# Layer 0's expert stage: when the fetched rows of the second expert table are multiplied

## The chip, the cores and the metric

One core of a Trainium2 chip runs one program. Its engines work in parallel and wait for each other through semaphores: PE (TensorE, matmuls into PSUM), DVE (VectorE), ACT (ScalarE), POOL (GpSimd) and SP (SyncE, here only a queue that issues transfers). Sixteen DMA engines carry all transfers. The metric is the device time of one execution in microseconds (us), lower is better.

## What is computed

Two layers; each is a token mixer followed by an expert layer (PEER). Only layer 0's expert layer matters here. It handles 256 latent tokens and 256 context tokens, 1024 wide. For every token, 8 heads pick 16 of 16384 experts each; an expert is one row of a first table (u) and one row of a second table (v):

```
q = t @ w_q                                    # 8 heads, two half keys each
best, pos = top_k(cand, 16); eidx = ...        # 128 experts per token
g = softmax(best)
act = gelu(einsum("thkd,td->thk", u_tab[eidx], t))
w = g * act
out = einsum("thk,thkd->td", w, v_tab[eidx])   # this document's subject
x = x + gate * out
```

## The kernel before

In layer 0 one half of the tokens (the latents, called "own" here) is computed densely: all 16384 experts, with the unchosen ones given weight zero. The other half (the context, called "far" in the code) is computed from rows that are fetched one by one with indirect DMAs on POOL's queue. The two are interleaved in one program whose order is written out by hand; every engine runs its instructions in that order.

The layer's stages, by items that `run` calls one after the other:

- `up(i)`, 128 items: the dense product with the first table, one block of 128 experts each. Beside it run the top-k of all tokens and `far_up`, which fetches rows of the first table (`u_rows`).
- `experts(t4)`, 64 items, the **selection stage**: four tokens each. `one_hots` (lines 1346 to 1352) makes masks on ACT, DVE and POOL, two items ahead; PE multiplies them into `psG` (line 1364, four matmuls); DVE multiplies the result into `A` (line 1366).
- `down(i)`, 128 blocks in 127 items, the **down stage**: the dense product with the second table, 24 matmuls a block (lines 200 to 202, into `acc`). Its 512 KB of table come in by SP's queue (line 113, tiles `raw`, three deep) and are split into a high and a low part (`whl`, lines 174 to 178, five deep).

The far half's product with the second table is `far_down`: 64 **steps**. A step needs four gathers of 128 rows (`fetch`, line 1219, four POOL instructions) into a set of four buffers; DVE spreads the weights (`wl`, line 1401) and PE does eight matmuls into `psC` (line 1413). The rows of the next step are ordered from inside the step: ahead of the step's matmuls if they go to another set of buffers, behind them if they go to the same set. There are three sets: `own` (in traces `hb`), `lent` (in traces `fetched`; these are the buffers of `whl`, so the down stage can't split its table before they are given back) and, from down block 16 on, rows 0 to 15 of `A`, which the down stage has used up by then. So in the selection stage two sets alternate; from there to block 16 there is one set alone; after that two again. After step 31 and after step 63, sixteen tile columns are moved out, transposed (`psX`, line 1429) and added to the context stream. The move behind step 31 is held back until block 28 (line 1421), as it writes into `A`. Behind step 63 come statistics and normalisation for layer 1 (`far_end`).

`far_go(want)` advances `far_down` until it has yielded `want` times; the first yield only orders the rows of step 0. `EARLY` is the number of steps that run in the selection stage, 24 in layer 0 (6 in layer 1). `far_go` is called at the end of each item: line 1373 in the selection stage, with at most one step more than before, and line 1506 in the down stage.

Of the kernel before, what the change touches and what calls it, by code (L numbers as in the profile page):

```python
# [69 lines left out]
class Builder:  # L70
# [10 lines left out]
    LO_DOWN = "v"  # L81


    FAR, WQ, UP, SHARE, EARLY = (256, 96), (8.0, 3.5), (4.0, 1.9), (0.75, 0.6), (24, 6)

    def __init__(self, tc, t, out):
        self.tc, self.nc, self.t, self.out = tc, tc.nc, t, out
# [919 lines left out]
    def peer(self, l, seg, far):  # L1007
# [8 lines left out]
        two = far != seg  # L1016
        NF = self.FAR[l]
        off = 0 if two else NF
        N = S - off
# [4 lines left out]
        EARLY = self.EARLY[l]  # L1024
# [3 lines left out]
        hold = dict(i=-1)  # L1028
# [71 lines left out]
        def psT(shape, name):  # L1100
            return self.ps.tile(shape, F, tag="acc", name=name, bufs=4)
# [204 lines left out]
        def aside(cost, until=None):  # L1306

            hold["due"] += cost
            while until not in hold if until else hold["due"] > 0:
                c = next(hold["side"], None)  # L1310
                if c is None:
                    break
                hold["due"] -= c
# [17 lines left out]
        def one_hots(t4):  # L1331

            if t4 == 0:
                hold["oj"] = mp.tile([128, 4, 4, 128], F, tag="wh", name="oj")
                hold["oi"] = mp.tile([128, 2, 2, 2, 128], F, tag="cand", name="oi", bufs=1)
            oj = hold["oj"][:, t4 % 4]
            if t4 % 3:
                oi = [hold["oi"][:, t4 % 3 - 1, e] for e in range(2)]
            else:
                oi = [mp.tile([128, 2, 128], F, tag="tw", name="oi", bufs=2) for _ in range(2)]  # L1340
            tk = 4 * t4

            def of(r, e):
                return sel[:, r, tk + e:tk + e + 1]
            for e in (0, 2):
                nc.scalar.activation(oi[e // 2][:, 0], self.iota, AF.Abs, bias=of(3, e))
            for e in (0, 2):
                nc.scalar.activation(oi[e // 2][:, 0], oi[e // 2][:, 0], AF.Relu, bias=of(2, e), scale=of(4, e))
            for e in (1, 3):
                eng = nc.gpsimd if (e == 3 and t4 % 2 if two else e == 1) else nc.vector  # L1350
                eng.tensor_scalar(oi[e // 2][:, 1], self.iota, of(0, e), of(2, e), op0=OP.is_equal, op1=OP.mult)  # L1351
            nc.vector.tensor_tensor(oj, self.iota[:, None, :].to_broadcast([128, 4, 128]),
                                    sel[:, 1, tk:tk + 4, None].to_broadcast([128, 4, 128]), op=OP.is_equal)
            oh[t4] = (oj, oi)

        def experts(t4):

            def fn():
                if 0 < t4 < N // 4 - 2:
                    one_hots(t4 + 2)  # L1360
                ps = psT([128, 128, 4], "psG")
                oj, oi = oh.pop(t4)
                for e in range(4):
                    nc.tensor.matmul(ps[:, :, e], oj[:, e], oi[e // 2][:, e % 2], start=True, stop=True)  # L1364
                a = A[:, :, 4 * t4:4 * t4 + 4]
                self.later(lambda: nc.vector.tensor_mul(a, a, ps))  # L1366
                last = t4 == N // 4 - 1
                if "up" not in hold:
                    aside(1e6 if last else 2.5)
                if "up" in hold:  # L1370
                    if "far" not in hold:
                        hold["far"], hold["done"] = far_steps(), 0
                    far_go(EARLY if last else min(hold["done"] + 1, EARLY * (t4 + 1) // (N // 4 - 4)))
                if t4 == N // 4 - 1:
                    self.flush()
                    self.lo_by = self.LO_DOWN
            return Item(fn)
# [76 lines left out]
        def far_steps():  # L1454
            yield from far_down()
            if two:
                yield from far_end()

        def far_go(want):

            while hold["done"] < want and next(hold["far"], False):
                hold["done"] += 1
# [3 lines left out]
        def w_halves(i):  # L1466
            at = i % 4
            hi, lo = wh[:, 0, at:at + 2], wh[:, 1, at:at + 2]
            self.halves(hi, lo, A[:, i:i + 2, :])
            wt[i] = (hi[:, 0], lo[:, 0])  # L1470
            wt[i + 1] = (hi[:, 1], lo[:, 1])

        FAR = 64 + 4 + 1 + 4 + 1 + 8 if two else nf + 3

        def down(i, n=1):

            def fn(*ps):
                nonlocal wh
                hold["i"] = i
                if i == 0:  # L1480
                    hold.pop("oj")
                    hold.pop("oi")
                    hold["acc"] = [psT([128, 2, 256], "acc") for _ in range(4)]
                    if two:
                        wh = mp.tile([128, 2, 4, 256], R, tag="wh", name="wh")
                        w_halves(0)
                if two:
                    if i % 2 == 0 and i < 126:
                        w_halves(i + 2)
                    if i == 28:  # L1490
                        hold["xf"] = A[:, 20:28]
                        nc.sync.dma_start(out=hold["xf"], in_=self.xs[far])
                    if i == 36:
                        hold["x"] = A[:, 28:36]
                        nc.sync.dma_start(out=hold["x"], in_=self.xs[seg])
                for d in range(8):
                    for j, p in enumerate(ps):
                        acc, first, last = hold["acc"][d // 2][:, d % 2, :N], i == 0 and d % 2 == 0, i + j == 127
                        if two:
                            self.mm3(acc, p.block(d), wt[i + j], first, last, skip=True)  # L1500
                        else:
                            nc.tensor.matmul(acc, p.raw[:, d * 128:d * 128 + 128], A[:, i + j], start=first, stop=last,  # L1502
                                             skip_group_check=True)
                for j in range(n):
                    wt.pop(i + j, None)
                far_go(EARLY + (FAR - EARLY) * (i + 1) // 122)
            return Item(fn, *[Piece(t["peer_v"][l, j * 128:j * 128 + 128], 1024, split=two, ring=ring) for j in range(i, i + n)],
                        ahead=i + n < 128)

# [158 lines left out]
```

## Time and profile before

| what | us |
|---|---|
| median of 3 runs (3422.04 to 3438.25) | 3436.36 |
| the profiled execution | 3428.33 |
| its span | 3426.6 |
| PE busy in the span | 3136.2 (92%) |
| DVE busy | 1892.8 (55%) |
| POOL busy | 1245.3 (36%) |
| ACT busy | 1077.7 (31%) |
| gathers of the second table into `hb`, `A`, `fetched` (line 1219): instructions | 140, 68, 48 |

A timeline row gives the start in us, the duration, the engine, the source line, the operation, "written<-read" tiles and the count of merged instructions; in brackets stands the idle time before it and what ended it. One matmul of fp32 is two instructions in the trace, so the four of a selection block are "x8" and the eight of a step "x16". Durations of matmuls overlap, since they are pipelined: what one costs is read from the distance of starts. The granted clock of PE is a share of 2.4 GHz.

### The profile page before, as it was taken

To read this page: it belongs to the slowest core of one execution; us is meant where nothing else is said; L and a number is where in the kernel's file an instruction comes from. 1 tells how busy PE (TensorE), PEld (TensorE's weight loads), DVE (VectorE), ACT (ScalarE), POOL (GpSimd) and SP (SyncE) were. 2 spreads that over 40 slices of the span, in tenths; PEclk is the share of its full clock that TensorE was granted. 3 is DMA by queue.
4 is the path that set the end of the run, shared out by engine and by line. 5 is a ranking of instruction groups with operands and counts; after the bars stand their busy time and mean duration, and the time that the engine had idled before them with its cause. 6 is when DMAs were issued, how large, how long until landed. Compare 5 with 4: busy or idle time off the path is not lost. (4 is left out here: it accounts for less than half of the span.)

```text
span 3426.6 us, 50779 instructions
## 1 busy us (share of the span) xinstructions
PE 3136.2 (92%) x19130; PEld 2516.7 (73%) x19130; DVE 1892.8 (55%) x4591; ACT 1077.7 (31%) x2268; POOL 1245.3 (36%) x1178
## 2 busy tenths in 40 slices
PE   7999999997899998578899998889999999979998
PEld 4667766785688887335577898567878889868897
DVE  5557444435899997755244456556444767660001
ACT  4544444421101101344233345554554111160000
POOL 2422222220254445675334411334553044463220
PEclk9999999998999999699999998999999999999999
DMA  7432222234699999887789966542335699969995
GB/s 267 159 97 62 65 57 60 91 116 157 251 398 391 376 397 407 311 286 246 257 311 395 396 231 204 174 142 84 97 103 153 218 375 408 400 202 327 350 353 186
DMA packets 245013, 819.03 MB, mean 239 GB/s; under 512 B 31776, under 2 KB 50464, under 8 KB 244512
## 3 DMA queue, kind: packets, MB, share of 16 engines
q1 hardware_dynamic: 137824, 441.40, 37.1%
q0 software_dynamic: 101376, 369.14, 28.9%
q10 hardware_dynamic: 5568, 5.24, 0.5%
q8 instruction: 151, 2.47, 0.3%
q14 instruction: 94, 0.77, 0.1%
HBM read 809.37 MB, written 6.29 MB: 238 GB/s over the span
## 5 line engine op out<-in xcount | busy, mean ns | idle before, releaser
L178 POOL TENSOR_TENSOR whl<-raw,whl 128x512 fp32r<-128x512 f32 x249 | 324.7, 1319 | 836.8 <-ACT whl L174 752.0
L176 DVE TENSOR_TENSOR whl<-raw,whl 128x512 fp32r<-128x512 f32 x359 | 277.8, 780 | 389.5 <-ACT whl L174 386.9
L1321 PE MATMUL psA<-hb,raw 128*128 128x256 f32 x2048 | 458.5, 383 | 9.1 <-DMA raw<-peer_u 7.0
L174 ACT ACTIVATE whl<-raw 128x512 fp32r<-128x512 f32 x608 | 363.4, 626 | 324.2 <-PE acc L202 273.7
L1321 PEld LDWEIGHTS psA<-hb,raw 128*128 128x128 f32 x2048 | 383.9, 190 | 76.7 <-issue 8.1
L200 PE MATMUL psA<-hhi,whl 128*128 128x512 f32 (+1 forms) x1032 | 377.0, 365 | 10.6 <-ACT hhi L505 8.0
L201 PE MATMUL psA<-hlo,whl 128*128 128x512 f32 (+1 forms) x1032 | 366.5, 355 | 0.9 <-POOL hlo L506 0.5
L202 PE MATMUL psA<-hhi,whl 128*128 128x512 f32 (+1 forms) x1032 | 365.1, 354 | 0.7 <-DVE whl L176 0.7
L200 PE MATMUL acc<-wh,whl 128*128 128x256 f32 x1024 | 296.3, 289 | 6.0 <-ACT wh L205 6.0
L1219 POOL DMA_INDIRECT fetched<-u_rows,ft x184 | 183.4, 997 | 317.9 <-PE psA L1321 136.5
L201 PE MATMUL acc<-wh,whl 128*128 128x256 f32 x1024 | 291.8, 285 | 0.1
L202 PE MATMUL acc<-wh,whl 128*128 128x256 f32 x1024 | 291.3, 284 | 0.0
L1323 ACT ACTIVATE A<-psA 128x512 f32<-128x512 f32 (+1 forms) x128 | 66.2, 517 | 686.8 <-PE psA L1321 686.8
L200 PEld LDWEIGHTS psA<-hhi,whl 128*128 128x128 f32 x1032 | 199.4, 193 | 61.2 <-issue 25.7
L1250 DVE SCALAR_TENSOR_TENSOR fetched<-fetched,hT 128x1024 f32<-128x1024 f32 x184 | 221.1, 1208 | 20.5 <-DMA fetched<-u_rows,ft 18.5
L200 PEld LDWEIGHTS acc<-wh,whl 128*128 128x128 f32 x1024 | 197.9, 193 | 40.9 <-issue 23.8
L202 PEld LDWEIGHTS psA<-hhi,whl 128*128 128x128 f32 x1032 | 199.4, 193 | 27.5 <-DVE whl L176 1.3
L201 PEld LDWEIGHTS psA<-hlo,whl 128*128 128x128 f32 x1032 | 199.1, 193 | 26.2 <-DVE hlo L393 1.1
L1219 POOL DMA_INDIRECT hb<-peer_v,ft x140 | 143.9, 1028 | 185.3 <-PE psC L1413 151.5
L201 PEld LDWEIGHTS acc<-wh,whl 128*128 128x128 f32 x1024 | 198.0, 193 | 0.4 <-DVE wh L206 0.4
L202 PEld LDWEIGHTS acc<-wh,whl 128*128 128x128 f32 x1024 | 198.0, 193 | 0.0
L1219 POOL DMA_INDIRECT own<-u_rows,ft x96 | 106.5, 1110 | 242.4 <-DVE own L1250 98.1
(372 smaller groups left out, 6052.3 us busy)
## 6 DMA issues: line engine op xcount, KB each, us to landing
raw<-peer_u SPq DMA_DIRECT2D x176, 512.0 KB, 6.9
raw<-peer_v SPq DMA_DIRECT2D x176, 512.0 KB, 6.6
raw<-w_in SPq DMA_DIRECT2D x126, 512.0 KB, 3.7
ring<-w_mod SPq DMA_DIRECT2D x88, 512.0 KB, 5.4
fetched<-peer_u SPq DMA_DIRECT2D x80, 512.0 KB, 11.6
fetched<-peer_v SPq DMA_DIRECT2D x80, 512.0 KB, 6.9
raw<-w_branch SPq DMA_DIRECT2D x32, 512.0 KB, 3.7
raw<-w_out SPq DMA_DIRECT2D x16, 512.0 KB, 3.7
```

What stands on the lines that cost most here:

```text
L174: nc.scalar.activation(hx, x, AF.Copy)
L176: nc.vector.tensor_sub(lx, x, hx.bitcast(F))
L178: nc.gpsimd.tensor_sub(lx, x, hx.bitcast(F))
L200: mm(ps, wh, xh, start=start, stop=False, skip_group_check=skip)
L201: mm(ps, wh, xl, start=False, stop=False, skip_group_check=skip)
L202: mm(ps, wl, xh, start=False, stop=stop, skip_group_check=skip)
L1219: nc.gpsimd.indirect_dma_start(out=buf, out_offset=None, in_=rows, in_offset=bass.IndirectOffsetOnAxis(ap=idx.bitcast(I32), axis=0))
L1250: nc.vector.scalar_tensor_tensor(b, b, 1.0, h, op0=OP.mult, op1=OP.mult, accum_out=f[:, 3, k:k + 1])
L1321: nc.tensor.matmul(ps[:, :N], p.raw[:, k * 128:k * 128 + 128], h32[:, k, off:], start=k == 0, stop=k == 7)
L1323: nc.scalar.activation(A[:, i - 1:i + 1, :], hold["ps"][:, :, :N], AF.Gelu_apprx_tanh)
```

## The change

Layer 0's `EARLY` goes from 24 to 18. With it, the number of steps that run in the selection stage goes from 24 to 18 (`far_go` counts one yield more than steps, and the old formula went past `EARLY` by one; the new one writes `EARLY + 1` out). In the down stage the six steps that are left over are spread by a new rule: up to block 16 one step in four blocks, after that evenly up to the count of 82 yields at block 121. Before, it was even from block 0 on. Layer 1 has `slow = 0`, so its rule for the down stage stays; its selection stage, where six yields made five steps, now goes to seven yields, that is six steps: one step moves from down block 5 to the selection stage there, and five selection blocks stand between steps instead of six.

```diff
-    FAR, WQ, UP, SHARE, EARLY = (256, 96), (8.0, 3.5), (4.0, 1.9), (0.75, 0.6), (24, 6)
+    FAR, WQ, UP, SHARE, EARLY = (256, 96), (8.0, 3.5), (4.0, 1.9), (0.75, 0.6), (18, 6)
...
-                    far_go(EARLY if last else min(hold["done"] + 1, EARLY * (t4 + 1) // (N // 4 - 4)))
+                    far_go(EARLY + 1 if last else min(hold["done"] + 1, (EARLY + 1) * (t4 + 1) // (N // 4 - 4)))
...
-                far_go(EARLY + (FAR - EARLY) * (i + 1) // 122)
+                slow = 4 if two else 0
+                far_go(EARLY + (i + 1) // 4 if i < 4 * slow else
+                       EARLY + slow + (FAR - EARLY - slow) * (i + 1 - 4 * slow) // (122 - 4 * slow))
```

In numbers: before, steps 24 to 31 followed down blocks 4, 6, 8, 10, 12, 14, 16 and 18, then none until block 28, which had two; step 63 followed block 90. Now steps 18, 19 and 20 follow blocks 7, 11 and 15, step 21 block 17, and from there a step follows every second block, with nine places where it follows the very next one (23 and 24, 30 and 31, 46 and 47, 53 and 54, 60 and 61, 67 and 68, 76 and 77, 83 and 84, 90 and 91); step 31 follows block 35, its transposes block 38, step 32 block 40, step 63 block 95.

PE in the middle of the selection stage (`psG` are the selection's matmuls, four a block; `psC` those of a step), before:

```order
L1364 MATMUL psG<-oi,oj 128x128 x12
L1413 MATMUL psC<-fetched,wl 32x512 x8
L1364 MATMUL psG<-oi,oj 128x128 x8
L1413 MATMUL psC<-hb,wl 32x512 x8
L1364 MATMUL psG<-oi,oj 128x128 x12
```

and now:

```order
L1364 MATMUL psG<-oi,oj 128x128 x12
L1413 MATMUL psC<-hb,wl 32x512 x8
L1364 MATMUL psG<-oi,oj 128x128 x16
L1413 MATMUL psC<-fetched,wl 32x512 x8
L1364 MATMUL psG<-oi,oj 128x128 x12
```

Two and a half blocks stood between steps, and now there are three, now and then four.

DVE at the end of the selection stage (line 176 subtracts for `whl`, which needs the lent buffers back; line 206 makes the first operand of the down stage), before:

```order
L1366 TENSOR_TENSOR A<-A,psG 128x128x4
L1401 TENSOR_TENSOR wl<-ft,zero_6371 128x128
L1366 TENSOR_TENSOR A<-A,psG 128x128x4
L176 TENSOR_TENSOR whl<-raw,whl 128x512 x2
L1366 TENSOR_TENSOR A<-A,psG 128x128x4 x2
L206 TENSOR_TENSOR wh<-A,wh 128x512 x2
```

and now:

```order
L1401 TENSOR_TENSOR wl<-ft,zero_6371 128x128
L1366 TENSOR_TENSOR A<-A,psG 128x128x4
L176 TENSOR_TENSOR whl<-raw,whl 128x512 x2
L1351 TENSOR_SCALAR oi<-iota,sel 128x128 x2
L1352 TENSOR_TENSOR oj<-iota,sel 128x512
L1366 TENSOR_TENSOR A<-A,psG 128x128x4
L1351 TENSOR_SCALAR oi<-iota,sel 128x128
L1352 TENSOR_TENSOR oj<-iota,sel 128x512
L1366 TENSOR_TENSOR A<-A,psG 128x128x4 x4
L206 TENSOR_TENSOR wh<-A,wh 128x512 x2
```

The last step follows block 59 instead of block 62, so four selection blocks instead of one come behind it, and the first splits of the down stage's table stand among them.

POOL where the selection stage ends and the down stage begins (every "x4" of line 1219 is the rows of one step), before:

```order
L1219 DMA fetched<-peer_v,ft 128x1024 x4
L1351 TENSOR_SCALAR oi<-iota,sel 128x128
L1219 DMA hb<-peer_v,ft 128x1024 x4
L178 TENSOR_TENSOR whl<-raw,whl 128x512 x3
L1219 DMA hb<-peer_v,ft 128x1024 x24
L1219 DMA A<-peer_v,ft 128x1024 x4
```

and now:

```order
L1219 DMA fetched<-peer_v,ft 128x1024 x4
L1351 TENSOR_SCALAR oi<-iota,sel 128x128 x2
L1219 DMA hb<-peer_v,ft 128x1024 x4
L178 TENSOR_TENSOR whl<-raw,whl 128x512 x3
L1351 TENSOR_SCALAR oi<-iota,sel 128x128
L1219 DMA hb<-peer_v,ft 128x1024 x12
L1219 DMA A<-peer_v,ft 128x1024 x4
```

With the one set `hb`, six steps' rows were fetched behind one another; now three are.

## Rows read from the trace of the kernel before

**Rows 1.** Busy time by stretch: window, length, engines (instructions), PE clock, DMA share, GB/s.
```profile
1420.00:1592.80 172.80, 141.59 (x824) 66.39 (x824) 94.46 (x211) 78.10 (x214) 123.37 (x121) 0.98 0.82 280
1624.10:1708.70 84.60, 66.75 (x385) 41.43 (x384) 21.13 (x37) 18.28 (x30) 27.03 (x28) 0.90 0.73 259
1767.90:1997.90 230.00, 228.96 (x1866) 183.49 (x1864) 104.56 (x177) 90.09 (x148) 111.02 (x108) 1.00 1.01 393
1598.80:1997.90 399.10, 373.03 (x2816) 289.33 (x2816) 162.18 (x276) 138.68 (x229) 157.78 (x156) 0.96 0.88 331
```
**Rows 2.** Who waited for whom, 1420 to 1592: us, times, longest.
```profile
PEld psC L1413 <- DMA hb<-peer_v,ft: 44.7, 28, 2.6
```
**Rows 3.** Timeline of the selection stage, PE and POOL.
```profile
1449.04 2.94 PE L1364 MATMUL psG<-oi,oj 128*128 128x128 f32 x24
...
1525.41 2.94 PE L1364 MATMUL psG<-oi,oj 128*128 128x128 f32 x24
1527.94 1.02 POOL L1219 DMA_INDIRECT hb<-peer_v,ft  x1 [0.17 <-issue]
1531.77 0.94 POOL L1219 DMA_INDIRECT hb<-peer_v,ft  x1 [0.30 <-issue]
1537.52 1.90 PE L1413 MATMUL psC<-hb,wl 128*32 128x512 f32 x10 [0.66 <-DMA hb<-peer_v,ft]
...
1584.63 2.94 PE L1364 MATMUL psG<-oi,oj 128*128 128x128 f32 x24
```
**Rows 4.** Timeline, end of the selection stage: a DVE row and PE's first row after.
```profile
1591.56 5.33 DVE L176 TENSOR_TENSOR whl<-raw,whl 128x512 fp32r<-128x512 f32 x2 [3.77 <-ACT whl L174]
...
1598.80 0.58 PE L200 MATMUL acc<-wh,whl 128*128 128x256 f32 x1 [6.01 <-ACT wh L205]
```
**Rows 5.** Timeline of PE, steps 25, 26 and 31 of the down stage.
```profile
1624.13 1.05 PE L1413 MATMUL psC<-hb,wl 128*32 128x512 f32 x2
1630.60 1.91 PE L1413 MATMUL psC<-hb,wl 128*32 128x512 f32 x10 [1.34 <-DMA hb<-peer_v,ft]
1638.38 1.18 PE L1413 MATMUL psC<-hb,wl 128*32 128x512 f32 x4
1644.79 2.43 PE L1413 MATMUL psC<-hb,wl 128*32 128x512 f32 x10 [0.50 <-DMA hb<-peer_v,ft]
...
1708.71 1.92 PE L1413 MATMUL psC<-A,wl 128*32 128x512 f32 x16
```
**Rows 6.** Timeline of PE, the transposes behind step 31, and step 35.
```profile
1739.46 1.03 PE L1429 MATMUL psX<-ident,A 128*128 128x128 f32 x8
...
1767.97 1.92 PE L1413 MATMUL psC<-A,wl 128*32 128x512 f32 x16
```
**Rows 7.** Timeline of PE, step 36, thirty matmuls apart in a block, step 63.
```profile
1775.77 1.92 PE L1413 MATMUL psC<-hb,wl 128*32 128x512 f32 x16
...
1840.05 0.28 PE L202 MATMUL acc<-wh,whl 128*128 128x256 f32 x1
1843.65 0.28 PE L202 MATMUL acc<-wh,whl 128*128 128x256 f32 x1
...
1997.91 1.92 PE L1413 MATMUL psC<-A,wl 128*32 128x512 f32 x16
```
**Rows 8.** DMA queues and issues, 1760 to 1990: packets, MB; count, us to landing.
```profile
q0 software_dynamic: 16248, 59.16, 65.9%
raw<-peer_v SPq DMA_DIRECT2D x58, 512.0 KB, 7.0
hb<-peer_v,ft POOLq DMA_INDIRECT x56, 7.6
A<-peer_v,ft POOLq DMA_INDIRECT x56, 8.0
```
**Rows 9.** One stretch of layer 1's expert layer, columns as in rows 1.
```profile
2960.00:2980.00 20.00, 17.39 (x116) 15.62 (x114) 3.87 (x8) 3.23 (x6) 2.82 (x3) 1.00 1.03 409
```
**Rows 10.** One stretch of layer 1's selection stage, columns as in rows 1.
```profile
3060.00:3080.00 20.00, 15.73 (x116) 11.90 (x114) 16.59 (x34) 15.35 (x45) 17.67 (x17) 0.91 0.57 187
```

## Prediction

> **What bounds the kernel now.** I read the busy time by stretch first [rows 1]. From 1420 to 1592.8, the selection stage, no engine is full: PE 142 of 173 us, POOL 123, DVE 94, and the DMA engines move 280 GB/s. From 1598.8 to 1997.9, the down stage with its steps, there are two regimes: up to 1708.7 PE is busy for 66.8 of 84.6 us at a mean granted clock of 0.90; from 1767.9 on it is busy for 229 of 230 us, at full clock, with the DMA engines at 393 GB/s. So the early part has room on every engine, and the late part on none.
>
> What PE waits for in the selection stage is the gathered rows: PE's weight loads for the steps alone wait 44.7 us for `hb` [rows 2]. The timeline shows the loop. It starts anew with the three selection blocks behind a step on `hb`, at 1449.04 and at 1584.63, nine pairs of steps apart: 135.6 / 18 = **7.53 us a step** [rows 3]. In the pair from 1525.41 to 1539.4, POOL issues the four gathers from 1527.94 on, 1.28 us apart, the last at 1531.77; PE's last part of that step gets its data at 1537.52 and takes 1.9 us. That is 2.5 us until POOL gets to issue, 3.8 of issue, 5.7 of landing and 1.9 on PE: all of it belongs to the gathers, and none to the two or three blocks between.
>
> **The selection stage.** Six steps fewer at 7.53 us are 45.2 us. Two things come back. A pair of steps now holds 6.33 selection blocks instead of 5. If the loop hides them all, this is free; if each of the 0.67 blocks more per step shows with DVE's whole time (94.5 us for about 55 blocks [rows 1], 1.7 us), 13 steps (those behind the start-up) lose 13 x 0.67 x 1.7 = 15 us. I take 4: PE waits for data at the end of the loop [rows 2, 3], which covers a block, but POOL also does one mask in every second block (line 1351), about 1 us, between its gathers: 13 x 0.33 x 1. Then four blocks instead of one follow the last step. A block takes PE 0.98 us (2.94 for three [rows 3]) and DVE 1.7; DVE does them behind the two subtractions of line 176, which take 5.33 us before the first down matmul at 1598.80 already [rows 4]. Three blocks cost 3 to 5 us; I take 4. Sum: -45 + 4 + 4 = **-37 us**, bounds -45 and -25.
>
> **The down stage before.** Its work must be priced to see its waits. Thirty matmuls run from 1840.05 to 1843.65 [rows 7], 0.12 us each, so 24 make a block of 2.88 us. From 1767.97 [rows 6] to 1775.77 [rows 7] lie two blocks and one step: 7.80 - 5.76, so a step costs PE 2.03 us. From 1598.80 [rows 4] to 1997.91 [rows 7] are 91 blocks and 39 steps, 262.1 + 79.2, and 1.0 of transposes [rows 6]: 342 us of 399, so 57 us are lost. Of them 37.8 lie between 1624.13 and 1708.71: 84.6 us for six gaps of two blocks and a step (6 x 7.79 = 46.8) [rows 5]. There only `hb` is fetched into, so the rows of a step are ordered when the step before is done: step 25 ends at 1632.5, step 26 has its last rows at 1644.79, **12.3 us**, where two blocks cover 5.8. Another 12.8 lie between the transposes at 1739.46 and step 35 at 1767.97 [rows 6], where two steps and the addition to the context stream are bunched at block 28: 28.5 us for three blocks, three steps and the transposes (15.7). The remaining 6 are the start at half clock, about 3, and one late set, about 3.
>
> **The down stage after.** Six steps more on PE: 6 x 2.03 = +12.2. The two losses above and the late set go: -37.8 - 12.8 - 2.9 = -53.5. What is late next? Steps 19 and 20 come four blocks behind the one before: 11.5 us, and the last rows are needed 0.7 later, so against 12.3 they wait 0 to 0.5 each; I take +1. Step 21 comes two blocks behind step 20 and its rows still go to the same set: one gap as before, 37.8 / 6 = +6.3. From block 17 to 95 the steps are denser: 43 steps and 78 blocks. The DMA engines must move 43 x 2.113 MB (59.16 MB for 28 steps, 112 gathers [rows 8]) + 78 x 0.524 + 2.1 for the two streams of lines 1492 and 1495 = 133.9 MB. Layer 1 shows a ceiling: 409 GB/s with PE at 17.4 of 20 us [rows 9]. At 409 this takes 327.4 us; PE needs 78 x 2.88 + 43 x 2.03 + 1 = 313. So **DMA becomes the bound there, by 14 us**. In the other view, each of the nine one-block gaps leaves a set 2.88 + 2.03 + 5.76 = 10.7 us, while issue (4 x 1.28) and landing (7.6 to 8.0 [rows 8]) want about 12: some 1.4 us each, 13 in all. I take +13; bounds 4 (the blocks split ahead absorb the rest) and 27 (the ceiling 393 of rows 1 instead of 409 makes 340.7). Sum: +12.2 - 53.5 + 1 + 6.3 + 13 = **-21 us**, bounds -30 and -7.
>
> POOL's queue past which gathers are moved: in the down stage it holds nothing else, so what waits behind a late gather is only the next one. SP's queue is unchanged up to eight stores of layer 1's input, and `far_end` reaches the count of 82 at block 121 as before; cost nothing, covered by 30 blocks of PE work behind step 63. Layer 1: one step moves into the selection stage, where POOL is busy for 17.67 of 20 us [rows 10]; its four gathers cost there at most 4 x 1.28 = 5 us, and its 2.03 on PE leaves the down stage: between -2 and +3, I take +1.
>
> **A rule that speaks against the change.** Rows 9 put the ceiling at 409 GB/s. The Trainium skill, "DMA: Bandwidth & Descriptors", section "Where 436 GB/s comes from", says that HBM binds a core's transfers at about 358 GB/s. By that rule (an estimate from its figure) the 133.9 MB take 374 us, 47 more than at 409, and the whole change would come to -10. The trace disagrees: 393 GB/s over 230 us and 409 in a stretch [rows 1, 9].
>
> **The sum.** -37 - 21 + 1 = -57 on the profiled execution of 3428.3: 3371. The median of the three runs is 3436, and the four times shown lie from 3422 to 3438 around 3432; I add 4, half of the distance between the median and the profiled execution: **3375 us**.
>
> **Rivals**, each by its sum against the forecast's -57:
> - A, the selection blocks are not hidden: DVE and PE work through the extra blocks in the open (DVE's 1.7 us each). For it: PE waits also for DVE's `wl` behind three blocks; against: DVE is busy only 94 of 173 us. Selection gives -25, the whole -45: 3387. Chance 0.14.
> - B, the late stretch eats the early gain: rows come late at most gaps, and the half clock that follows a long wait (0.90 in the early stretch [rows 1]) comes on top. Then the down stage gives about 0, the whole -36: 3396. For it: 393 GB/s with PE full leaves nothing to give [rows 1]; against: 409 is reachable. Chance 0.12.
> - C, the fetches' lateness is absorbed and the blocks are free: -45 - 30 + 1 = -74: 3358. Chance 0.06.
> - D, a ceiling between the down stage's mean and 393: at the figure where selection and early down just pay, 133.9 MB must take 57 us longer than 327.4, that is 348 GB/s. The time then stays at 3432, and within 0.5% of it for 334 to 364 GB/s. The skill's HBM rule above would be this case; the rows speak against it. Chance 0.04.
> - E, slower: gathers of 128 scattered rows mixed with table loads hold only the mean of the whole down stage, 331 GB/s [rows 1]. 133.9 MB then take 404.5 us, 77 more: 3428 - 57 + 77 + 4 = 3452. It is slower from 348 GB/s down, by over 0.5% from 334. For it: the selection stage's gathers move 280; against: there POOL's issue and PE's loop space them out, and the late stretch holds 393 with 28 steps in it [rows 1, 8]. Chance 0.03.
> - The change does not do what it says: the order of instructions shows 18 steps and the new spacing, so nothing is left for that.
>
> **How the numbers follow.** Forecast 0.61. A measurement tells about 0.5% (17 us) from no change. Faster by more: forecast, A, B and C, 0.93; within: D, 0.04; slower: E, 0.03. The range takes in the bounds of the unknown costs, -45 - 30 and -25 - 7 with layer 1's +1, that is 3358 to 3401, and with them A, B and C; the runs' own spread adds a little: 3354 to 3402. D and E are left out.
>
> **What would show it.** In the profile after, the first matmul of `acc` starts near 1562 instead of 1598.8; steps in the selection stage are 7.5 to 7.9 us apart; PE's waits for `hb` between blocks 4 and 18 shrink to one of 5 to 6 us at step 21, and no bunch of steps stands behind the transposes; from block 17 to 95 the DMA engines hold 400 to 410 GB/s and PE waits about 1.4 us at each one-block gap; step 63 starts near 1954 instead of 1997.9, though it stands five blocks later in the order (five blocks and its own start: 1997.9 + 14.4 - 58). Wrong would be: a step spacing above 8.5 us (A), waits of several us at most steps in the late stretch (B, E), or a rate stuck near 350 GB/s (D).

## The result, and the profile after

The changed kernel takes **3394.97 us** (median, 3385.26 to 3399.17) against 3433.57 for the kernel before, measured beside it: 38.6 us faster by the medians. The ratio of the runs is 0.9899, 95% interval 0.9874 to 0.9925, which is 35 us, 26 to 43. The forecast was 3375, a gain of 57 to 59. So the direction holds and the time lies in the range, near its upper end; a third of the gain or more did not come.

The profiled execution took 3395.13 us, its span is 3393.4 us, and 33.2 us separate it from the profiled one of before. They lie as follows (a plus is time lost). "Equal blocks" allows for step 63 standing five blocks later, 5 x 2.88 us; the work of the six steps more, 12.2 us, is not taken off.

| stretch | forecast | measured |
|---|---|---|
| up to step 0, same instructions in both | 0 | +4.7 |
| step 0 to the first matmul of `acc` | -37 | -30.3 (178.8 became 148.5) |
| first `acc` to step 63, at equal blocks | -21 | -4.3 (399.1 + 14.4 became 409.2) |
| layer 1, selection +2.4 and down stage -2.2 | +1 | +0.2 |
| the rest, between the layers | 0 | -3.4 |

The lines with the same instructions, the first and the last, moved by several us and nearly cancel; nothing is read from them. Of the whole miss, the down stage holds 17 us and the selection stage 7.

Busy time by stretch of the kernel after, with the columns of [rows 1]: selection; down stage to step 21; step 21; to the transposes; the late stretch with its seven later one-block gaps; the whole from `acc` to step 63.

```profile
1424.70:1561.80 137.10, 112.97 (x696) 59.46 (x696) 87.26 (x197) 72.98 (x204) 101.59 (x95) 0.97 0.77 259
1573.20:1634.40 61.20, 59.28 (x481) 53.61 (x482) 30.88 (x49) 26.52 (x44) 12.51 (x13) 1.00 0.67 223
...
1634.40:1650.10 15.70, 10.85 (x65) 6.54 (x64) 2.94 (x7) 3.04 (x5) 7.83 (x8) 1.00 0.98 357
...
1650.10:1734.50 84.40, 80.37 (x617) 60.45 (x617) 34.15 (x57) 30.16 (x50) 40.31 (x40) 1.00 0.99 382
1743.10:1982.40 239.30, 228.76 (x1816) 173.71 (x1816) 98.70 (x169) 82.85 (x137) 121.28 (x120) 1.00 0.99 385
1573.20:1982.40 409.20, 386.10 (x3032) 300.99 (x3032) 172.35 (x294) 145.49 (x241) 181.93 (x180) 1.00 0.94 359
```

The early stretch, where before PE was busy for 66.8 of 84.6 us at a clock of 0.90 [rows 1], now has PE at 59.3 of 61.2 and at full clock: the loss that the change aimed at is gone, but for one set at step 21, below. But the late stretch, full before (229.0 of 230.0, 393 GB/s [rows 1]), now has PE idle for 10.5 of 239.3 us, and the rate fell to 385. The forecast had 400 to 410 there.

Where PE idles in the late stretch, and what a set's rows need: timeline of the kernel after, around the one-block gap of steps 39 and 40 (columns: start, duration, engine, line, operation, in brackets the idle time before and what ended it).

```profile
1789.16 1.92 PE L1413 MATMUL psC<-A,wl 128*32 128x512 f32 x16
...
1791.34 0.95 POOL L1219 DMA_INDIRECT A<-peer_v,ft  x1 [2.77 <-PE psC L1413]
...
1795.23 1.16 POOL L1219 DMA_INDIRECT A<-peer_v,ft  x1 [0.30 <-issue]
...
1796.95 1.92 PE L1413 MATMUL psC<-hb,wl 128*32 128x512 f32 x16
...
1801.87 1.06 PE L1413 MATMUL psC<-A,wl 128*32 128x512 f32 x6
1804.10 1.90 PE L1413 MATMUL psC<-A,wl 128*32 128x512 f32 x10 [1.18 <-DMA A<-peer_v,ft]
1811.87 1.92 PE L1413 MATMUL psC<-hb,wl 128*32 128x512 f32 x16
```

The set `A` comes free when its step ends at 1791.1. POOL issues its four gathers from 1791.34 to 1795.23, and the last rows let PE go on at 1804.10: 13.0 us after the set came free, 8.9 after the last issue began. The window, the time from the end of the step that frees a set to the start of the next step that reads it, is 10.7 here. From 1801.87 to 1811.87 are 10.0 us where two blocks and a step are 7.79: 2.2 lost here. Over the nine one-block gaps, priced in this way, it is 27 us, 2.2 to 3.2 each and 6.4 at the one (blocks 30 and 31) beside the load of the context stream (line 1492). A second profile of the same kernel has 23 us at the nine.

The one set that still waits in the early part, step 21 (timeline of PE, after):

```profile
1634.35 1.04 PE L1413 MATMUL psC<-hb,wl 128*32 128x512 f32 x2
1637.15 1.05 PE L1413 MATMUL psC<-hb,wl 128*32 128x512 f32 x2 [1.76 <-DMA hb<-peer_v,ft]
1639.52 1.04 PE L1413 MATMUL psC<-hb,wl 128*32 128x512 f32 x2 [1.32 <-DMA hb<-peer_v,ft]
1642.34 1.90 PE L1413 MATMUL psC<-hb,wl 128*32 128x512 f32 x10 [1.77 <-DMA hb<-peer_v,ft]
1650.11 1.92 PE L1413 MATMUL psC<-A,wl 128*32 128x512 f32 x16
```

From 1634.35 to 1650.11 are 15.76 us for the same 7.79 of work: 8.0 lost, forecast 6.3. PE takes the rows one by one as they land, and five more waits like it were there before [rows 5].

The end of the selection stage, after, with two of DVE's, one of POOL's and three of PE's rows:

```profile
1561.76 0.69 DVE L176 TENSOR_TENSOR whl<-raw,whl 128x512 fp32r<-128x512 f32 x1 [3.15 <-ACT whl L174]
1562.80 4.20 DVE L176 TENSOR_TENSOR whl<-raw,whl 128x512 fp32r<-128x512 f32 x1 [0.35 <-ACT whl L174]
```
```profile
1562.67 3.72 POOL L178 TENSOR_TENSOR whl<-raw,whl 128x512 fp32r<-128x512 f32 x3
```
```profile
1561.83 2.05 PE L1364 MATMUL psG<-oi,oj 128*128 128x128 f32 x16
1568.26 3.50 PE L1364 MATMUL psG<-oi,oj 128*128 128x128 f32 x16 [4.38 <-DVE oj L1352]
1573.20 0.38 PE L200 MATMUL acc<-wh,whl 128*128 128x256 f32 x1 [1.44 <-ACT wh L205]
```

DVE's second subtraction for `whl`, 0.69 us a moment earlier, takes 4.20 while POOL does three of the same kind; the masks of the last two of the four left selection blocks stand behind it on DVE, and PE waits 4.38 for them. From the last step to `acc` it is 11.3 us, before 7.1.

PE's waits for data in the selection stage, before (waits of the stretch 1420 to 1592) and after (1424 to 1562); us, times, longest:

```profile
PEld psC L1413 <- DVE wl L1401: 14.7, 19, 1.2
PE psC L1413 <- DVE wl L1401: 10.4, 16, 1.0
```
```profile
PEld psC L1413 <- DMA hb<-peer_v,ft: 19.5, 16, 3.3
...
PEld psC L1413 <- DVE wl L1401: 14.0, 13, 1.9
PE psC L1413 <- DVE wl L1401: 11.5, 13, 1.7
PEld psC L1413 <- DMA fetched<-peer_v,ft: 11.3, 11, 2.5
```

The waits for `hb`, 44.7 us over 24 steps before [rows 2], are 19.5 over 18. Those for DVE's `wl` are as long in sum as before, so per step they have grown, from 0.6 to 0.8 us of PE's weight loads.

### The profile page after: what moved, and what is told of

It is laid out like the page before. It is cut to its first block, busy times and chain, and to the rows that moved or that the text cites. A ratio compares the mean times of both kernels' runs of the same rounds, so it can differ in the third digit from the quotient of the medians.

```text
span 3393.4 us, 50776 instructions
## 1 busy us (share of the span) xinstructions
PE 3111.5 (92%) x19130; PEld 2514.0 (74%) x19130; DVE 1893.5 (56%) x4591; ACT 1076.3 (32%) x2268; POOL 1250.6 (37%) x1178
## 5 line engine op out<-in xcount | busy, mean ns | idle before, releaser
L1321 PE MATMUL psA<-hb,raw 128*128 128x256 f32 x2048 | 458.9, 383 | 14.6 <-DMA raw<-peer_u 12.7
L200 PE MATMUL psA<-hhi,whl 128*128 128x512 f32 (+1 forms) x1032 | 375.6, 364 | 10.5 <-DVE bones L459 6.6
```

The lines of the kernel that those rows point to most:

```text
L200: mm(ps, wh, xh, start=start, stop=False, skip_group_check=skip)
L1321: nc.tensor.matmul(ps[:, :N], p.raw[:, k * 128:k * 128 + 128], h32[:, k, off:], start=k == 0, stop=k == 7)
```

## The experiments

The theories at the start: **window** (a one-block gap gives a set 10.7 us, its rows want 13, so the places of the steps cost the time, and another spacing gives it back) against **ceiling** (the late stretch wants more bytes than the DMA engines can bring, so any spacing loses the same).

**A step every second block.** The same 18 steps in the selection stage; from block 17 on every gap is two blocks (four around the transposes), so step 63 moves from block 95 to 103.

```
-                far_go(EARLY + (i + 1) // 4 if i < 4 * slow else ...)
...
+                elif i < 16:
+                    far_go(EARLY + (i + 1) // 4)
+                elif i < 38:
+                    far_go(22 + (i - 15) // 2)
+                elif i < 41:
+                    far_go(min(i, 39) - 4)
+                elif i < 104:
+                    far_go(36 + (i - 41) // 2)
+                else:
+                    far_go(i - 36)
```

> The changed kernel, but from block 17 on every step follows the second block after the one before (step 63 behind block 105 instead of 95; the items behind it one per block). In the profile of the changed kernel the nine one-block gaps cost about 27 us: after such a gap the next pair of gaps takes 2.2 to 3.4 us more than its blocks and steps. Theory 1, the window: a set of buffers needs about 13 us from the end of the step that frees it to its last row, two two-block gaps give 13.5 and a one-block gap 10.7. Then the 27 us fall to under 5, and the time to about 3372 (23 less than the changed kernel). Theory 2, the loss sits elsewhere in the late stretch (the two 1 MB loads, the rows of the table, any dense stretch of 43 steps): at least half stays, 3382 to 3395.

Measured: 3357.64 us against 3424.34, ratio **0.9810** (0.9793 to 0.9826). Busy time by stretch of this kernel:

```profile
1743.10:1972.30 229.20, 229.20 (x1878) 183.89 (x1876) 105.12 (x177) 89.32 (x147) 117.96 (x114) 1.00 1.02 403
```

PE does not idle at all in the late stretch, and the DMA engines hold 403 GB/s where the changed kernel had 385. The window theory holds: the rate was there to be had, and of the 27 us (23 in the second profile) under 5 are left between steps 22 and 63. By the ratios this is some 27 to 30 us below the changed kernel, more than the 23 expected. In the profiles 20 to 22 of them lie between the first `acc` and step 63, at equal blocks; the rest lies in stretches with the same instructions and is within what the runs vary.

**A third set of buffers.** The changed kernel's spacing, but from block 54 on the rows 36 to 51 of `A` are a third set, and rows are ordered two steps ahead. Only the five later one-block gaps lie behind that; the earlier ones are a control.

```
+                sets = [own, lent[:4], [... (0, 4, 8, 12)], [flat(A[:, r:r + 4]) for r in (36, 40, 44, 48)]]
...
+                if two and hold["i"] >= 54 and s + 2 < len(steps):
+                    busy = [n] + [g for g, _ in got.values()]
+                    get(s + 2, [x for x in (0, 2, 3) if x not in busy][0])
```

> The changed kernel, its order of steps untouched, but from block 54 on a third set of four buffers (rows 36 to 51 of A), and rows are ordered two steps ahead. Same bytes, same steps. Five of the nine one-block gaps lie there; they cost 2.8, 3.2, 2.5, 2.2 and 2.8 = 13.5 us in the profile of the changed kernel. Window theory: the wait of a step on its rows goes, and those five cost under 3 us together (time about 3384). Ceiling theory (the DMA engines carry 409 GB/s at most, seven blocks and four steps need 12.1 MB, 29.6 us against 28.3 of PE): at least 1.3 us of each gap stays, 6.5 in all (time about 3388), and the rate in that stretch comes to 405 to 409 GB/s.

Measured: 3378.13, ratio 0.9862 (0.9842 to 0.9882). The two expected times lie 4 us apart, so only the profile can tell them apart. The five gaps lose 0.4, 1.9, 1.4, 1.5 and 1.7 us, 7 in all, where the changed kernel loses 13.5 at the same five; the two controls in the late stretch lose 2.9 and 3.1, there 2.2 each. Timeline of PE at a control and at a gap with the third set (its added lines make line 1413 line 1416), and the stretches that they lie in:

```profile
1798.03 1.91 PE L1416 MATMUL psC<-A,wl 128*32 128x512 f32 x10 [1.02 <-DMA A<-peer_v,ft]
```
```profile
1857.00 1.90 PE L1416 MATMUL psC<-A,wl 128*32 128x512 f32 x10 [0.90 <-DMA A<-peer_v,ft]
```
```profile
1826.00:1963.00 137.00, 134.66 (x1072) 101.64 (x1074) 57.71 (x100) 49.62 (x82) 70.66 (x70) 1.00 1.03 408
1743.00:1826.00 83.00, 81.16 (x634) 60.25 (x633) 33.61 (x59) 28.59 (x47) 46.81 (x46) 1.00 1.01 394
```

The rate of the first of these two stretches in 40 slices, and the time from issue to landing of its gathers:

```profile
GB/s 408 410 410 403 408 411 409 413 402 413 407 410 409 403 413 408 410 410 403 408 410 410 413 402 409 410 408 408 409 407 411 408 405 411 408 410 398 411 407 402
```
```profile
DMA to landing us min/median/max: 13.0/14.1/15.3
```

With rows ordered two steps ahead the wait is not the window's any more. The rate is 408 GB/s in nearly every slice, the ceiling that [rows 9] had shown at 409, and a gather that is issued earlier only takes longer, 14.1 us where [rows 8] has 7.6 to 8.0. So of some 13 us about half was the window and half the ceiling. At 1.4 us a gap, nine gaps would lose some 13 us (an estimate) that more buffers cannot give back at this spacing: the size of the prediction's term, and the cause that it gave first.

**Part 1 alone.** 18 steps in the selection stage, and the old even spacing from block 0 on.

```
-                far_go(EARLY + (i + 1) // 4 if i < 4 * slow else ...)
+                far_go(EARLY + (FAR - EARLY) * (i + 1) // 122)
```

> The first part of the change alone: 18 steps in the selection stage, the rest spread evenly from block 0 on as in the kernel before. Seven gaps of about two blocks then lie where only one set is fetched into, at 6.3 us each 44 us, against 10 in the changed kernel; in the late stretch only about four one-block gaps are left, 12 us instead of 27. Theory (both parts are needed): +19 on the changed kernel, 3414. Rival (the selection stage alone gives the gain): 3395.

Measured: 3400.89, ratio 0.9927 (0.9898 to 0.9957). The down stage is 12.6 us longer than before at equal blocks, and 12.2 of that is the work of its six steps more: its waits are as long as before. Timeline of PE at steps 21 to 23:

```profile
1614.65 1.54 PE L1413 MATMUL psC<-hb,wl 128*32 128x512 f32 x6
1617.47 1.90 PE L1413 MATMUL psC<-hb,wl 128*32 128x512 f32 x10 [1.28 <-DMA hb<-peer_v,ft]
1625.25 1.06 PE L1413 MATMUL psC<-hb,wl 128*32 128x512 f32 x4
1629.83 1.47 PE L1413 MATMUL psC<-hb,wl 128*32 128x512 f32 x2 [3.52 <-DMA hb<-peer_v,ft]
...
1642.33 1.52 PE L1413 MATMUL psC<-hb,wl 128*32 128x512 f32 x6
```

Step 21 to 22 takes 10.60 us and step 22 to 23 17.08, where 7.79 is their work; seven such gaps cost 41 us. So the four-block spacing is what removes these waits. By the ratios this part alone is some 10 to 13 us above the changed kernel, between the theory's 19 and the rival's 0, and their intervals overlap. The profile decides: its down stage takes 17 us more than the changed kernel's, at equal blocks.

**Part 2 alone, by the one number.** 24 steps were meant in the selection stage, with the new spacing:

```
-    FAR, WQ, UP, SHARE, EARLY = (256, 96), (8.0, 3.5), (4.0, 1.9), (0.75, 0.6), (18, 6)
+    FAR, WQ, UP, SHARE, EARLY = (256, 96), (8.0, 3.5), (4.0, 1.9), (0.75, 0.6), (24, 6)
```

> The second part of the change alone: still 24 steps in the selection stage (with the new formula, so the last one follows block 59), then one per four blocks up to block 16, then evenly. Selection stage: as before plus 4 us for four blocks behind the last step instead of one. Down stage: none of the 54 us of waits, except for one gap with a single set (8 us) and about 2 us at the four-block gaps; almost no one-block gaps (the rate is 0.51 steps a block), so no 27 us. Theory: 37 us less than the kernel before, 3396, the same as the whole change: what six steps save in the selection stage they give back in the late stretch. Rival (the steps in the selection stage carry the gain): 3415 or more.

Measured: 3386.6, ratio 0.9897 (0.9879 to 0.9915). It does not isolate the part: by the changed formula of line 1373 the selection stage does 25 steps here, not 24. It showed one thing by accident: with the last step reading `hb`, which is not lent, only 2.5 us lie between that step and `acc`, not 11.3.

**The changed kernel again, and part 2 alone with 24 steps.** The second has the line above and a bound in the selection stage:

```
-                    far_go(EARLY + 1 if last else min(hold["done"] + 1, (EARLY + 1) * (t4 + 1) // (N // 4 - 4)))
+                    far_go(EARLY + 1 if last else min(hold["done"] + 1, EARLY + 1, (EARLY + 1) * (t4 + 1) // (N // 4 - 4)))
```

> The changed kernel itself, for a second profile and for times beside those below. The selection stage took 148.5 us from the first step to the first matmul of the down stage in its first profile and 143.6 to 146.1 in three other kernels with the same stage, so some 144 to 148 are expected here; the nine one-block gaps again about 27 us, the gap behind step 21 about 8. Ratio to the kernel before 0.988 to 0.992.

> The second part alone, with 24 steps in the selection stage (the earlier run of this had 25, since 25 * 63 // 60 is 26 yields). Selection stage about 179 + 4 us. Down stage: 0.51 steps a block leave one one-block gap instead of nine; one gap with a single set (8 to 11 us), 2 to 4 at the start. About 40 us less than before in the down stage, 36 in all, ratio 0.989 to 0.990: as much as the whole change. If the gain came from the selection stage, the ratio would stay above 0.995.

Measured: 3391.6, ratio 0.9890 (0.9864 to 0.9915), for the changed kernel, and 3390.08, ratio 0.9899 (0.9873 to 0.9924), for part 2 alone: the same. The second profile of the changed kernel has 146.8 us from step 0 to `acc`, 23 us at the nine one-block gaps (27 were expected) and 10.4 at step 21 (8 expected). In part 2 alone the selection stage is as long as before (179.6 us from step 0 to `acc`), and the down stage is 35.6 us shorter at equal blocks. Its late stretch:

```profile
1747.80:1968.30 220.50, 218.96 (x1769) 172.01 (x1768) 99.19 (x167) 83.82 (x138) 109.15 (x108) 1.00 1.02 402
```

PE idles for 1.5 of 220.5 us, with 40 steps from `acc` to step 63 instead of 46. So each part by itself is worth 25 and 35 us, and both together 35 to 38: **some 20 us are lost where they meet**. The times alone would leave that open, with some 10 us of doubt on each of the three. The profiles put it in the down stage: +12.6 and -35.6 would make -23.0 there, and the two profiles of the changed kernel have -4.3 and -3.3. It is the down stage that must take the six steps, with nine one-block gaps where part 2 alone has one.

**Two-block spacing with a 19th selection step.** As the first experiment, with the accident of the fourth put to use: one more step in the selection stage, behind its block 62, and the last single-set step four blocks behind the one before.

```
+                        far_go(EARLY + 2 if last else min(hold["done"] + 1, (EARLY + 2) * (t4 + 1) // 63))
...
+                elif i < 16:
+                    far_go(EARLY + 1 + (i + 1) // 4)
+                elif i < 38:
+                    far_go(23 + max(i - 17, 0) // 2)
...
```

> The two-block spacing, and two more edits: the nineteenth step stays in the selection stage (behind block 62; it reads the other set, so the lent buffers come back while it waits and the first splits are done by then), and step 22, the last with a single set, follows four blocks behind the one before instead of two. In the two-block version the gap with the single set cost 10.9 us and the time from the last step to the first down matmul was 12.1. Theory: the gap falls to about 1, the tail to 3 to 8; 13 to 18 us less than the two-block version, ratio 0.976 to 0.978 (two-block version 0.981). Rival: the bound is POOL's and DMA's work in the selection stage, then the tail only moves into the step before and 9 us are gained, 0.9785.

Measured: 3358.61, ratio 0.9805 (0.9783 to 0.9828), the same as without the 19th step. Step 0 to `acc` is 147.7 us here with one step more, 143.6 there. Timeline of PE at its end:

```profile
1563.90 1.91 PE L1364 MATMUL psG<-oi,oj 128*128 128x128 f32 x8 [4.93 <-DVE oj L1352]
1566.07 2.59 PE L1416 MATMUL psC<-hb,wl 128*32 128x512 f32 x16 [0.26 <-DVE wl L1404]
```

The short tail is there (2.5 us), but PE now waits 4.9 us for DVE ahead of the last step, where the 4.75 us subtraction of line 176 stands: the wait moved, as the rival said. The gap at the last step with a single set fell from 10.9 to 1.9 us, and the down stage is 14 us shorter in the profile, 2 of it the step that moved. But the times show neither the theory's 13 to 18 us nor the rival's 9; the interval of the ratio still reaches the rival's 0.9785.

**The same with 15 selection steps.** Four fewer in the selection stage, two-block spacing to block 111.

```
-    FAR, WQ, UP, SHARE, EARLY = (256, 96), (8.0, 3.5), (4.0, 1.9), (0.75, 0.6), (18, 6)
+    FAR, WQ, UP, SHARE, EARLY = (256, 96), (8.0, 3.5), (4.0, 1.9), (0.75, 0.6), (14, 6)
...
+                elif i < 46:
+                    far_go(19 + max(i - 17, 0) // 2)
...
```

> The version with one step kept back, but 15 steps instead of 19 in the selection stage; every second block holds a step up to block 111. Theory of the loop (a step costs 7.5 to 7.9 us there whatever stands between): 4 x 7.7 = 31 less in the selection stage, 4 x 2.03 = 8 more in the down stage, 23 less than the version with 19. Rival, the selection blocks come into the open (4.2 blocks a step, DVE 1.7 us a block and PE behind it): the stage shrinks by half of that or less, and the whole gain is under 8 us.

Measured: 3357.26, ratio 0.9793 (0.9771 to 0.9816). The selection stage is 129.2 us, 18.5 less than with 19 steps where the theory had 31, and the down stage takes 13 us more of the same blocks where it had 8. The steps lie 8.7 us apart (from step 2 to step 12). Timeline of PE in the selection stage:

```profile
1489.73 3.84 PE L1364 MATMUL psG<-oi,oj 128*128 128x128 f32 x32
1494.91 1.93 PE L1416 MATMUL psC<-hb,wl 128*32 128x512 f32 x16 [1.34 <-DVE wl L1404]
1496.76 3.62 PE L1364 MATMUL psG<-oi,oj 128*128 128x128 f32 x30
...
1502.17 1.94 PE L1416 MATMUL psC<-fetched,wl 128*32 128x512 f32 x6 [0.50 <-DVE wl L1404]
1504.34 1.90 PE L1416 MATMUL psC<-fetched,wl 128*32 128x512 f32 x10 [0.22 <-DMA fetched<-peer_v,ft]
```

With four blocks to a step PE's weight loads wait 1.0 us a step for DVE's `wl` and 1.2 for the rows, where the kernel before has 0.6 and 2.2: the blocks now show. Three spacings give the curve, each counted from step 2 on: 7.3 and 7.5 us a step at 2.4 to 2.5 blocks a step (part 2 alone, the kernel before), 7.8 to 8.1 at three (six profiles), 8.7 at four. The time is that of the 18 and the 19 steps within the intervals, so nothing is shown to be gained by fewer selection steps beyond this point.

The three kernels with two-block spacing, 3357 to 3359 us, beat both the kernel before (by 65 to 71 us) and the changed one (by some 30).

## Why the prediction was right and where it was wrong

- **What bounds the kernel: right.** The early waits came from the single set and the bunch at block 28: part 1 alone brings single-set waits back, part 2 alone takes 35.6 us off the down stage. Behind the transposes no bunch stands any more (step 32 follows with 1.8 us of wait).
- **The selection stage, -37: right in kind, -30 in size.** Its terms: six steps at 7.53 us hold. The return for the denser blocks was taken as 4 (0.3 us for each of 13 steps); the steps lie 8.12 us apart in this profile (from step 2 to step 16), 7.8 to 8.1 in four others with the same selection stage, so 3 to 8 us. The four blocks at the end cost 4.2, forecast 4. The start-up, step 0 to step 2, cost 2.7 more (11.2 us, before 8.5). In the other profiles the stage takes 143.6 to 146.8 us, a gain of 32 to 35: the term was nearly right, and this execution lay at its poor end. The sign "a spacing above 8.5" for rival A did not come at 18 steps; at 15 it did, with 8.7.
- **The down stage, -21: wrong, -4.3, outside even its bounds of -30 to -7.** The step that failed is **the +13 for the one-block gaps**: "issue and landing want about 12: some 1.4 us each". They cost 27 us, 3.0 each (23 and 2.6 in the second profile). Two things were wrong in the term. Its own numbers, 4 x 1.28 and 7.6 to 8.0, add up to 12.7 to 13.1 and not to about 12, which against the window of 10.7 would have been 2.0 to 2.4 a gap. And landing was taken as the median over all gathers [rows 8], where PE waits for the last of the four. The trace of the kernel before held that already: in the late stretch its 28 sets land 6.6, 7.5, 8.6 and 9.2 us after the issue (medians of the first to the fourth gather), and from the first issue of a set to its last landing it is 13.1 us. In the gap shown above it is 0.3 until POOL issues, 3.9 to the last issue and 8.9 to its landing: 13.0, and 2.3 a gap where the rows alone decide. The upper bound of 27 had been worked out from another cause (a ceiling of 393 GB/s), and met the number by luck. The smaller terms make the rest of the miss, under 3 us together: step 21 cost 8.0, forecast 6.3; the two four-block gaps 2.4, forecast 1; the wait behind the transposes 1.7, forecast 0; the start 0.8, where the prediction had left about 3.
- **The range: in part luck.** It adds up the bad ends of the two stages, -25 and -7. The down stage went past its end, and the time is inside because the selection stage came near its forecast.
- **"DMA becomes the bound there": half right.** The prediction gave 13 us in two views, a ceiling of 409 GB/s and a window, and took them for one and the same. They are two limits: in the changed kernel the window binds (385 GB/s), and a third set reaches the ceiling of 408, and with the wider spacing PE is full at 403. Rate by slices of the late stretch, after:

```profile
GB/s 213 330 405 400 403 412 401 385 387 405 389 413 394 396 391 399 411 359 371 398 400 359 374 359 407 409 410 408 410 373 377 391 399 411 397 401 381 409 409 276
```

  Around 410 between the gaps, with slices down to 359 (and lower at both ends of the stretch): not one steady rate at a limit, as the third set's is. The DMA share of 0.99 there is no limit either; it is 1.03 at 408 GB/s.
- **The rivals.** B's time came (3396 forecast for it, 3395 measured), with its down stage "about 0". Of its mechanism the first half is what happened, rows that come late, though at nine gaps and not at most; the other half, the half clock, did not come: the clock is 1.00 in the whole down stage (0.98 in the second profile). It had 0.12, and deserved more, since 1.6 us more a gap, with the smaller terms above, was enough for it. A: at 18 steps the blocks show by 0.2 to 0.6 us a step, not by 1.1. C came nowhere. D and E fall: 403 to 408 GB/s were held. By the rule of the Trainium skill, "DMA: Bandwidth & Descriptors", section "Where 436 GB/s comes from", about 358 GB/s would be the end; the runs disagree, with 385 to 408 GB/s in the late stretches of all ten profiles.
- **Layer 1, +1**: +0.2, within what the runs vary.

That the early loss was that of the single set and the bunch, that the late one is the window's and then the ceiling's, and that the parts meet with a loss of some 20 us is shown by the runs; how the early loss divides between the set and the bunch is read from the timeline alone. Why the last gather of a set lands later than the first was not isolated. A rate near 400 GB/s is not needed for it: in the early down stage of before, at 259 GB/s, the first lands after 4.5 us and the last after 8.2 (medians of eight sets). Why the same selection stage takes 143.6 in one profile and 148.5 in another stays open.

## What to carry to other kernels

Price a prefetch by its last piece: from the end of the step that frees the buffer to the landing of the last transfer, read off at the load that the changed kernel will have there, and compare that with the shortest gap between two uses, not with the mean one. Work moved from a stage that waits to one that is full has to be spread so that no gap falls below that time: here evenly rounded gaps of one and two blocks lost 27 us where an equal spacing of two, which ends eight blocks later, lost under 5. When a change has two parts, test each alone: here one gave 25 us and the other 35, and both together no more than 38.

## What the runs showed of the hardware

- The indirect gathers of 128 rows landed 5.7 us after the issue in the selection stage at 280 GB/s [rows 1, 3], and 8.9 for the last of a set in the late stretch of after at 385. In the late stretch of before, at 393, the four of a set took 6.6, 7.5, 8.6 and 9.2 (medians).
- One core's DMA engines held 403 GB/s over 229 us and 408 over 137.
- DVE's subtraction of 128x512 values took 0.69 us alone and 4.20 beside three of the same kind on POOL; [rows 4] shows 5.33 for two. In three profiles (before, after, the 19th step) DVE's ends 0.6 us behind the last of POOL's three, as if it had waited for all of them; what they share was not isolated.
- Stretches with the same instructions differ by several us between executions: step 0 started from 1416.3 to 1426.6 in the profiles, so a term of 5 us can't be told from one profile.
